# Attention values in 512-column sets, units and gate blocks spread between the projections of an encoder trunk

## The chip, the core and the metric

The kernel runs on one core of one Trainium2 chip. Such a core has TensorE (PE, matrix products into PSUM), VectorE (DVE, elementwise work and reductions), ScalarE (ACT, activations and copies), GpSimd (POOL) and SyncE (SP, which here issues nearly all DMA transfers). SBUF is the working memory with 128 partitions; PSUM holds products in banks of 128 x 512 float32.

The metric is the device time of one execution in microseconds (us); for a kernel it is the median of several runs. A profile is of one execution.

## What is computed

Two layers of an encoder trunk for 512 tokens and a model width of 1024, all in float32. In a layer three mixers run on the same normalized input and are merged by gates, then come a feed-forward part and a gated per-layer input:

```python
h = rmsnorm(x, norm_mix[i])
proj = h @ w_in[i]
qa, ka, va, glu_in, qc, kc, vc, gates = jnp.split(proj, SPLITS, axis=-1)
ya = diff_attention(qa, ka, va, ...)          # 4 heads of two 64-wide halves, values 128 wide
yb = conformer_conv(glu_in, conv_w[i], ...)   # z = a * sigmoid(g), 31 taps, layernorm, silu
yc = neighbourhood_attention(qc, kc, vc, rpb[i])   # 8 heads of 64, on an 8 x 64 grid
ga, gb, gc = jnp.split(jax.nn.sigmoid(gates), 3, axis=-1)
merged = ga * (ya @ w_br_a[i]) + gb * (yb @ w_br_b[i]) + gc * (yc @ w_br_c[i])
x = x + merged @ w_o[i]
h = rmsnorm(x, norm_ffn[i])
x = x + (silu(h @ w_ffn_gate[i]) * (h @ w_ffn_up[i])) @ w_ffn_down[i]
h = rmsnorm(x, norm_ple[i])
x = x + sigmoid(h @ w_ple_gate[i]) * (p[i] @ w_ple_in[i])
```

After the two layers a last `rmsnorm` gives the output. The widths that matter below: `va` and `vc` are 512 columns each, `glu_in` is 2 x 512, `gates` is 3 x 1024.

## The kernel before

**Numbers in two parts.** A float32 operand is kept as a high part (type fp32r, a copy by ScalarE) and a low part (the rest, a subtraction by VectorE); `split` (L162) makes both. A product of two operands is three products on TensorE: high by high, high by low, low by high (`mm3`, L175). `weights` (L166) loads a block of 128 x 1024 weights by SP into a `wr` buffer and splits it into `wh` and `wl`, three buffers of each, with a higher priority than the work around it.

**A projection** is `gemm` (L181): 8 blocks of the contraction, three products each, 24 products of 512 columns (the tokens) into one PSUM bank, which another engine then empties. Activations lie transposed, so a projection gives 128 channels by 512 tokens. `values` (L561) is the exception: it gives tokens by channels, 128 tokens at a time, with the activations as the stationary operand and the weights as the moving one. It makes 256 columns (half of the heads) in a call, 96 products of 256 columns into two banks, and is called four times in a layer: `natten_v(0)`, `natten_v(1)`, `diff_v(0)`, `diff_v(1)`.

**The order of the work.** TensorE's instructions run in the order in which the program issues them (a manual schedule). The order on the other engines is found by a scheduler when the kernel is built, by priority (mostly the order in the program) and by when inputs and buffers come free; within an engine it is then fixed. A buffer has a tag with a number of copies (L293): `v` 4, `y` 5, `z` 5, `x` 4, `t` 7, `rp` 2, `qk` 2, `b` 2, `r` 3, `a` 3, `e` 2; of the eight PSUM banks `mm` has 3, `sc` 2, `tr` 2 and `av` 1.

**Ticks.** Attention is cut into units that are put between the projections. `chunk` (L115) is called after each three products of a projection, and every fourth call is a tick (`tick`, L94): 12 products of 512 columns. At a tick those generators go on whose time has come (`yield 2` is two ticks later), and one more unit is started from the queue. `later(gen, delay, gap)` puts a unit in the queue: it starts at the earliest `delay` ticks later, and the next one at the earliest `gap` ticks after it.

- `natten_in(pr)` projects q and k of two of the 8 neighbourhood heads. SP copies the parts into the stacked buffers `qk` and `x` (12 copies). Four units follow, `natten_unit` (L643): scores on TensorE (`natten_sc`, L762), bias and minimum on VectorE, the exponential on ScalarE; two ticks later transposes (`natten_tr`, L683 to L687), split by ScalarE and VectorE into `natten_pt`; two ticks later the product with the values (`natten_av`, L704 and L705) in the one `av` bank, which ScalarE and VectorE empty into `natten_y`. Two units of a half share the bank. L705 uses edge values, which SP copies to the other partitions after `values`.
- `diff_in(head)` does the same for a head of the differential attention, with the rotary embedding between (VectorE, and four copies by SP for each of q and k). Its units are `diff_unit` (L796): scores (`diff_sc`, L762), and for every second unit three ticks later transposes and two ticks after that `diff_av`, also in the `av` bank, then a norm at the end of a head.

**A layer** (L413): four gated blocks of the convolution's input (`glu`, two projections each), which start before the norm's row factors `rb` are known and are scaled by them on the way out of PSUM. `scaled` (L241) then makes eight normalized operands h[0] to h[7] on VectorE and ScalarE, one a tick; all later projections use these. Then head pair 0 of the neighbourhood attention, `natten_v(0)`, pairs 1 and 2, `natten_v(1)`, pair 3, differential head 0, `diff_v(0)`, head 1, one gate block of the third kind (`gate_c`), head 2, `diff_v(1)`, head 3, the other seven `gate_c`, two `gate_b`, all sigmoids so far, `branch_c` (8 blocks of 12 products), two `gate_b`, `merge_a` (8 x 36 products), and the convolution's norm between four `gate_b`. The first two gated blocks of the first layer are made in `opening`, while the input loads.

**Convolution taps.** The 124 taps of a layer (31 for each of four blocks `z`) are one VectorE instruction each (L160, `conv_z`). They are not placed by the program's order alone: `background(after, n)` (L515) issues the next `n` of them and lets them start no sooner than `after`. `BG` (L51) has the numbers for each kind of work; `conv` issues what is left before it takes the mean.

## Time and profile before

| | |
|---|---|
| median of 3 runs | 1796.83 us (1795.61 to 1800.21) |
| the profiled execution | 1793.92 us |
| its span, first to last instruction | 1792.1 us |
| TensorE busy | 1778.6 us, 10404 products |
| VectorE busy | 1381.7 us |
| ScalarE busy | 895.0 us |
| TensorE's granted clock | 1.000 |
| read from HBM | 216.44 MB, 125 GB/s with what is written |

How it is read: a tile is named by its phase and tag, so `natten_pt` is a buffer of tag `pt` that the phase `natten` made, and an instruction is written out<-in. L12 is line 12 of the kernel; a line can be that of a helper, such as L143 (any activation), L157 (any `tensor_tensor`) or L177 to L179 (the three products of `mm3`). In the timeline a row has the start, the length, the engine and what it does; `x3` are three instructions of one kind merged, and brackets give how long the engine stood idle before it and what ended that. Products are pipelined: the next one starts before the one ahead is drawn to end. In the waits view a row has who waited, for whom, the total in us, how many times, and the longest. In the stages below, layer 0 lies at 28 to 438 us up to the merge, and the same stage of layer 1 some 888 us later.

### The profile page before, as it was taken

Reading aid. Unit: us, or ns where it says so; the run is one execution under the profiler, and the core shown is the slowest. Engines: PE = TensorE matmul, PEld = TensorE weight load, DVE = VectorE, ACT = ScalarE, POOL = GpSimd, SP = SyncE. Lnnn points to the kernel's source line nnn. Section 1 sums busy time; section 2 is a strip of 40 time slices with the busy share of each in tenths; the row PEclk is TensorE's granted clock in tenths of the full one; section 3 lists DMA queues with packets and bytes.
Section 4 is the critical chain, followed back from the end, with each engine's and each line's share of the span. In section 5 each row is a group of like instructions: output and inputs, shape, how many; then the busy total and the mean of one; then the engine's idle time right before and its main releaser. Section 6 shows DMA issues by size and latency. Waiting matters only on the chain. (4 is left out here: it accounts for less than half of the span.)

```text
span 1792.1 us, 27370 instructions
## 1 busy us (share of the span) xinstructions
PE 1778.6 (99%) x10404; PEld 1571.3 (88%) x10404; DVE 1381.7 (77%) x2142; ACT 895.0 (50%) x1499; POOL 63.5 (4%) x102
## 2 busy tenths in 40 slices
PE   9999999999999999999999999999999999999998
PEld 7888888888899899898878888888888998998987
DVE  7888887897877577577787878878878775765776
ACT  5576555325565245255545755553256652542544
POOL 0000000000000000000000000000000100000000
PEclk9999999999999999999999999999999999999999
DMA  6666561325656466253437655523364762763432
GB/s 201 171 191 167 145 159 42 111 90 156 214 142 185 138 155 187 83 140 120 159 117 194 187 152 161 128 63 100 97 192 146 194 180 84 195 169 112 118 111 92
DMA packets 98963, 257.56 MB, mean 144 GB/s; under 512 B 13072, under 2 KB 18576, under 8 KB 98832
## 3 DMA queue, kind: packets, MB, share of 16 engines
q1 hardware_dynamic: 91344, 231.19, 42.4%
q0 software_dynamic: 6336, 23.07, 7.3%
q8 instruction: 82, 1.34, 0.3%
q10 hardware_dynamic: 1152, 1.55, 0.3%
q14 instruction: 49, 0.40, 0.1%
HBM read 216.44 MB, written 7.86 MB: 125 GB/s over the span
## 5 line engine op out<-in xcount | busy, mean ns | idle before, releaser
L143 ACT ACTIVATE ffn_wh<-ffn_wr 128x1024 fp32r<-128x1024 f32 (+1 forms) x114 | 117.3, 1029 | 184.1 <-PE ffn_mm L178 99.5
L160 DVE SCALAR_TENSOR_TENSOR conv_z<-glu_z,pre_par,conv_z 128x512 f32<-128x512 f32 x240 | 179.2, 747 | 2.9
L157 DVE TENSOR_TENSOR ffn_wl<-ffn_wr,ffn_wh 128x1024 fp32r<-128x1024 f32 (+1 forms) x114 | 134.9, 1183 | 49.9 <-ACT ffn_wh L143 49.5
L1049 PE MATMUL ffn_sc<-wo_h,ffn_wh 128*128 128x256 f32 x704 | 130.4, 283 | 0.0
L1049 PEld LDWEIGHTS ffn_sc<-wo_h,ffn_wh 128*128 128x128 f32 x704 | 110.4, 192 | 0.8
L1049 PE MATMUL ffn_sc<-wo_h,ffn_wl 128*128 128x256 f32 x352 | 99.6, 283 | 0.0
L177 PE MATMUL ffn_mm<-ffn_z,ffn_wh 128*128 128x512 f32 x240 | 93.4, 389 | 0.0
L178 PE MATMUL ffn_mm<-ffn_z,ffn_wh 128*128 128x512 f32 x240 | 93.4, 389 | 0.0
L179 PE MATMUL ffn_mm<-ffn_z,ffn_wl 128*128 128x512 f32 x240 | 93.4, 389 | 0.0
L157 DVE TENSOR_TENSOR ffn_t<-ffn_mm,wo_r 128x512 f32<-128x512 f32 x48 | 33.1, 689 | 67.8 <-PE ffn_mm L179 67.8
L157 DVE TENSOR_TENSOR ffn_wl<-ffn_rp,ffn_wh 128x1024 fp32r<-128x1024 f32 x44 | 53.7, 1221 | 30.3 <-ACT ffn_wh L143 30.3
L143 ACT ACTIVATE mergea_wh<-mergea_wr 128x1024 fp32r<-128x1024 f32 (+1 forms) x32 | 27.1, 846 | 96.8 <-PE mergea_mm L178 70.8
L1049 PEld LDWEIGHTS ffn_sc<-wo_h,ffn_wl 128*128 128x128 f32 x352 | 67.5, 192 | 0.0
L1049 PE MATMUL ffn_sc<-wo_qk,ffn_wh 128*128 128x256 f32 x352 | 67.1, 283 | 0.0
L1049 PE MATMUL ffn_sc<-wo_v,ffn_wh 128*128 128x256 f32 x352 | 67.1, 283 | 0.0
L1049 PE MATMUL ffn_av<-wo_h,ffn_wh 128*128 128x256 f32 x352 | 65.3, 283 | 0.0
L143 ACT ACTIVATE ffn_wh<-ffn_rp 128x1024 fp32r<-128x1024 f32 x44 | 46.4, 1055 | 29.6 <-PE ffn_mm L178 17.5
L1049 PEld LDWEIGHTS ffn_sc<-wo_qk,ffn_wh 128*128 128x128 f32 x352 | 54.9, 192 | 0.0
L1049 PEld LDWEIGHTS ffn_av<-wo_h,ffn_wh 128*128 128x128 f32 x352 | 54.9, 192 | 0.0
L1049 PEld LDWEIGHTS ffn_sc<-wo_v,ffn_wh 128*128 128x128 f32 x352 | 54.9, 192 | 0.0
L179 PEld LDWEIGHTS ffn_mm<-ffn_z,ffn_wl 128*128 128x128 f32 x240 | 45.1, 188 | 9.3
L178 PEld LDWEIGHTS ffn_mm<-ffn_z,ffn_wh 128*128 128x128 f32 x240 | 45.1, 188 | 9.2
(688 smaller groups left out, 5785.9 us busy)
## 6 DMA issues: line engine op xcount, KB each, us to landing
ffn_wr<-w_gu SPq DMA_DIRECT2D x66, 512.0 KB, 4.3
ffn_e<-w_gu SPq DMA_DIRECT2D x32, 512.0 KB, 3.6
ffn_e<-w_gu POOLq DMA_DIRECT2D x32, 512.0 KB, 7.5
ffn_wr<-w_fd SPq DMA_DIRECT2D x32, 512.0 KB, 4.4
natten_wr<-w_in SPq DMA_DIRECT2D x16, 512.0 KB, 4.6
natten_b<-bias SPq DMA_DIRECT2D x32, 256.0 KB, 2.9
diff_wr<-w_in SPq DMA_DIRECT2D x16, 512.0 KB, 3.8
gatec_wr<-w_in SPq DMA_DIRECT2D x16, 512.0 KB, 4.2
```

Source lines behind the costliest of these rows:

```text
L143: i = self.nc.scalar.activation(out, in_, func, **kw)
L157: return self.nc.vector.tensor_tensor(out, a, b, op)
L160: return self.nc.vector.scalar_tensor_tensor(out, a, s, b, op0, op1)
L177: mm(out, wh, ah, start=first, stop=False)
L178: mm(out, wh, al, start=False, stop=False)
L179: mm(out, wl, ah, start=False, stop=last)
L1049: mm(bank[:, u], w[:, u, kp], t, start=begin and n == 0, stop=False, skip_group_check=True)
```

## The change

What it does, part by part:

- **Values.** `values` makes all 512 columns in one call, so it is called once for the neighbourhood attention and once for the differential attention. It makes four sets of 128 tokens, in three `mm` banks and the `av` bank, with products of 512 columns. The contraction is walked in three steps (blocks 0 and 1, 2 and 3, 4 to 7), each over all four sets; each set is split as soon as its last product is done. The weights lie in memory in another order; the loads are as many and as large. All four `v` buffers hold one call. The edge values go to four `t` buffers in place of two `x`.
- **Units.** In place of delay 5 and gap 1, a neighbourhood head pair has delays 6, 4, 4, 4 and gaps 2, 2, 2, 1. In place of delay 7 or 6 and gap 2, a differential head has delay 8 (head 0) or 5, and gap 2, for head 3 gap 1.
- **The last gated block** moves from the start of the layer to between head pairs 1 and 2. It uses h, ScalarE copies both projections from PSUM, and `finish` applies the sigmoid and the product after the gate blocks.
- **Gate blocks** are spread: two `gate_c` after pair 2, one after differential head 0, `diff_v` after head 1, `gate_c` and two `gate_b` after head 2, and the rest after head 3. All four `gate_b` that came before `merge_a` now come before `branch_c`, in buffers of tags `b` and `rp`.
- **Taps.** Gated blocks of the first layer and its head pair 0 no longer issue taps, and the second call of a block in `merge_a` issues three in place of two.

```diff
...
 WARM = 10
-BG = dict(glu=2, natten=3, diff=1, gatec=2, branchc=1, gateb=5, mergea=4, mergea2=2)
+BG = dict(glu=2, natten=3, diff=1, gatec=2, branchc=1, gateb=5, mergea=4, mergea2=3)
 FIRST = (["v"] * 4 + ["pt"] * 2 + ["y", "b"], ["y"] * 5 + ["pt"] * 2 + ["b"])
...
         self.todo = self.taps(zs, cs)
-        self.glu(zs)
+        self.glu(zs, range(3))
         if i == 0:
...
         yc, ya, yb = [], [], []
+        acc, gb = [], []
+        self.ms = iter(range(KD)), iter(range(KD))
         sn, sd = {}, {}
...
         self.h = self.hs
-        self.natten_v(0, sn)
+        self.natten_v(sn)
         self.natten_in(1, sn, yc)
+        finish = self.glu_last(zs)
         self.natten_in(2, sn, yc)
-        self.natten_v(1, sn)
+        self.gates(acc, gb, "cc")
         self.natten_in(3, sn, yc)
-        acc, gb = [], []
         self.diff_in(0, sd, ya)
-        self.diff_v(0, sd)
+        self.gates(acc, gb, "c")
         self.diff_in(1, sd, ya)
-        self.gate_c(acc, 0)
+        self.diff_v(sd)
         self.diff_in(2, sd, ya)
-        self.diff_v(1, sd)
+        self.gates(acc, gb, "cbb")
         self.diff_in(3, sd, ya)
-        for m in range(1, KD):
-            self.gate_c(acc, m)
-        for m in range(2):
-            self.gate_b(gb, m, AF.Copy, None)
+        self.gates(acc, gb, "ccbbcc")
         for g in acc + gb:
             self.act(g, g, AF.Sigmoid, table="sigmoid")
+        finish()
         self.branch_c(acc, yc)
-        for m in range(2, 4):
-            self.gate_b(gb, m, AF.Sigmoid, "sigmoid")
         self.merge_a(ya, acc)
...
         return ps
-    def glu(self, zs):
+    def glu(self, zs, js):
         self.phase = "glu"
-        if not self.first:
+        if 0 in js and not self.first:
             self.first = [self.ps("mm") for _ in range(2)]
             self.pair(self.first, [self.a["w_in"][self.i, (OFF_GLU + o) // P] for o in (CB, 0)], self.h)
-        nc = self.nc
-        for j in range(4):
+        for j in js:
             sg, ta = self.sb("t", [P, 512]), self.sb("t", [P, 512])
...
             def value(j=j, pa=pa, sg=sg, ta=ta, z=z):
                 self.tt(ta, pa, self.rb, ALU.mult)
-                mid = z[:, HALO:HALO + GW, :]
-                zc = self.tt(mid.rearrange("p a b -> p (a b)"), ta, sg, ALU.mult)
-                nc.vector.memset(z[:, 0:HALO, 0:1], 0.0)
-                nc.vector.memset(z[:, HALO + GW:, GR - 1:GR], 0.0)
-                nc.vector.tensor_copy(z[:, 0:HALO, 1:GR], z[:, GW:GW + HALO, 0:GR - 1])
-                nc.vector.tensor_copy(z[:, HALO + GW:, 0:GR - 1], z[:, HALO:2 * HALO, 1:GR])
-                if j:
+                zc = self.gated(z, ta, sg)
+                if j and self.i:
                     self.background(zc, self.bg["glu"])
             self.ready(value)
+    def gated(self, z, a, g):
+        nc = self.nc
+        mid = z[:, HALO:HALO + GW, :]
+        zc = self.tt(mid.rearrange("p a b -> p (a b)"), a, g, ALU.mult)
+        nc.vector.memset(z[:, 0:HALO, 0:1], 0.0)
+        nc.vector.memset(z[:, HALO + GW:, GR - 1:GR], 0.0)
+        nc.vector.tensor_copy(z[:, 0:HALO, 1:GR], z[:, GW:GW + HALO, 0:GR - 1])
+        nc.vector.tensor_copy(z[:, HALO + GW:, 0:GR - 1], z[:, HALO:2 * HALO, 1:GR])
+        return zc
+    def glu_last(self, zs):
+        self.phase = "glu"
+        sg = self.sb("r", [P, 512])
+        z = self.sb("z", [P, GW + 2 * HALO, GR])
+        zs.append(z)
+        mid = z[:, HALO:HALO + GW, :].rearrange("p a b -> p (a b)")
+        for out, off in ((sg, CB), (mid, 0)):
+            self.act(out, self.proj(OFF_GLU + off + 3 * P), AF.Copy)
+        def finish():
+            self.act(sg, sg, AF.Sigmoid, table="sigmoid")
+            self.gated(z, mid, sg)
+        return finish
     def taps(self, zs, cs):
...
     def values(self, ap, parts):
         mm = self.nc.tensor.matmul
-        accs = [self.ps("mm", (P, 2, 256)) for _ in range(2)]
-        for o in range(0, KD, 4):
-            wh, wl = self.weights(ap[:, o * 256:(o + 4) * 256], 1024)
-            for k in range(o, o + 4):
-                s = slice((k - o) * 256, (k - o + 1) * 256)
-                for t in range(4):
-                    out = accs[t // 2][:, t % 2, :]
-                    ts = slice(t * P, (t + 1) * P)
-                    mm(out, self.h[k][:, 0, ts], wh[:, s], start=k == 0 and t % 2 == 0,
-                       stop=False, skip_group_check=True)
-                    mm(out, self.h[k][:, 0, ts], wl[:, s], start=False, stop=False,
-                       skip_group_check=True)
-                    mm(out, self.h[k][:, 1, ts], wh[:, s], start=False,
-                       stop=k == KD - 1 and t % 2 == 1, skip_group_check=True)
+        accs = [self.ps("mm") for _ in range(3)] + [self.ps("av")]
+        ws = []
+        def products(t, ks):
+            ts = slice(t * P, (t + 1) * P)
+            for k in ks:
+                wh, wl = ws[k // 2]
+                s = slice(k % 2 * 512, k % 2 * 512 + 512)
+                hi, lo = self.halves(self.h[k])
+                mm(accs[t], hi[:, ts], wh[:, s], start=k == 0, stop=False)
+                mm(accs[t], hi[:, ts], wl[:, s], start=False, stop=False)
+                mm(accs[t], lo[:, ts], wh[:, s], start=False, stop=k == KD - 1)
                 self.chunk()
-                self.chunk()
-        vs = []
-        for acc in accs:
-            v = self.sb("v", [P, 2, 512], F32R)
-            for t in range(2):
-                for hi, lo, a in parts(v[:, t], acc[:, t]):
-                    self.split(hi, lo, a)
-            vs.append(v)
-        return vs
+        for o in range(4):
+            ws.append(self.weights(ap[:, o * 1024:(o + 1) * 1024], 1024))
+        for ks in ((0, 1), (2, 3), (4, 5, 6, 7)):
+            for t in range(4):
+                products(t, ks)
+                if ks[-1] == KD - 1:
+                    v = self.sb("v", [P, 2, 512], F32R)
+                    for hi, lo, a in parts(v, accs[t]):
+                        self.split(hi, lo, a)
+                    accs.append(v)
+        return accs[4:]
     def natten_in(self, pr, st, ys):
...
             self.background(self.stt(low, ps, f, nat.bitcast(F32), ALU.mult, ALU.subtract),
-                            self.bg["natten"])
+                            self.bg["natten"] if pr or self.i else 0)
             self.stack(nat, low, st4[:, 2 * s:2 * s + 2], k2 if s else None)
...
         for n in range(4):
-            self.later(self.natten_unit(pr, n // 2, n % 2, st4, k2, st, box, ys[pr]), 5, 1)
+            self.later(self.natten_unit(pr, n // 2, n % 2, st4, k2, st, box, ys[pr]),
+                       (6, 4, 4, 4)[pr], (2, 2, 2, 1)[pr])
     def stack(self, nat, low, one, two):
...
                                                part[64 * u:64 * u + 64].bitcast(F32))
-    def natten_v(self, g, st):
+    def natten_v(self, st):
         self.phase = "natten"
         def parts(v, a):
-            v = v.rearrange("p (u a b c) -> p u a b c", u=2, b=2, c=64)
-            a = a.rearrange("p (u a c) -> p u a c", u=2, c=64)
-            return [(v[:, u, :, u], v[:, u, :, 1 - u], a[:, u]) for u in range(2)]
-        vs = self.values(self.a["w_vc"][self.i, g], parts)
-        vd = self.sb("x", [P, 2, 512], F32R)
-        for n, edge in enumerate((vs[1][0:64, 0], vs[0][64:P, 1])):
-            for o in range(0, P, 64):
-                self.nc.sync.dma_start(vd[o:o + 64, n].bitcast(F32), edge.bitcast(F32))
-        st["v", g] = vs, vd
+            v = v.rearrange("p g (u a b c) -> p u g a b c", u=2, b=2, c=64)
+            a = a.rearrange("p (g u a c) -> p u g a c", g=2, u=2, c=64)
+            return [(v[:, u, :, :, u], v[:, u, :, :, 1 - u], a[:, u]) for u in range(2)]
+        vs = self.values(self.a["w_vc"][self.i], parts)
+        vds = []
+        for g in range(2):
+            vds.append([self.sb("t", [P, 512], F32R) for _ in range(2)])
+            for vd, edge in zip(vds[g], (vs[2][0:64, g], vs[1][64:P, g])):
+                for o in range(0, P, 64):
+                    self.nc.sync.dma_start(vd[o:o + 64].bitcast(F32), edge.bitcast(F32))
+        st["v"] = vs, vds
     def natten_unit(self, pr, half, u, st4, k2, st, box, y):
...
         yield 2
-        vs, vd = st["v", pr // 2]
+        vs, vds = st["v"]
+        g = pr // 2
         if u == 0:
...
             for k in range(2):
-                mm(av, vs[half][:, n, cols], pp[:, k, n], start=n == k == 0, stop=False)
-        mm(av[:, ws], vd[:, half, cols], p2, start=False, stop=True)
+                mm(av, vs[2 * half + n][:, g, cols], pp[:, k, n], start=n == k == 0, stop=False)
+        mm(av[:, ws], vds[g][half][:, cols], p2, start=False, stop=True)
         qs = slice(half * 256, half * 256 + 256)
...
         self.tt(y[rs, 1, qs], y[rs, 1, qs].bitcast(F32), av[ro], ALU.add)
+    def gates(self, acc, gb, names):
+        for n in names:
+            if n == "c":
+                self.gate_c(acc, next(self.ms[0]))
+            else:
+                self.gate_b(gb, next(self.ms[1]), AF.Copy, None)
     def gate_c(self, acc, m):
...
         if m % 2 == 0:
-            gs += self.parts_of("v", [512], 2)
+            if m == 0:
+                gs += [self.sb("b", [P, 512]) for _ in range(2)]
+            else:
+                gs += self.parts_of("rp" if m == 2 else "v", [512], 2)
         self.background(self.act(gs[m], ps, func, table=table), self.bg["gateb"])
     def merge_b(self, ys, acc, gs):
...
         for qt in range(4):
-            self.later(self.diff_unit(head, qt, st4, k2, st, box, ys), 6 if head else 7, 2)
-    def diff_v(self, g, st):
+            self.later(self.diff_unit(head, qt, st4, k2, st, box, ys), 8 if head == 0 else 5,
+                       1 if head == 3 else 2)
+    def diff_v(self, st):
         self.phase = "diff"
-        st["v", g] = self.values(self.a["w_va"][self.i, g], lambda v, a: ((v[:, 0:256], v[:, 256:512], a),))
+        def parts(v, a):
+            return [(v[:, :, 0:256], v[:, :, 256:], a.rearrange("p (g c) -> p g c", g=2))]
+        st["v"] = self.values(self.a["w_va"][self.i], parts)
     def diff_unit(self, head, qt, st4, k2, st, box, ys):
...
             for u in range(2):
-                v = st["v", head // 2][kp][:, u].rearrange("p (a b) -> p a b", a=2)
+                v = st["v"][2 * kp + u][:, head // 2].rearrange("p (a b) -> p a b", a=2)
                 self.mm3(av[:, half * 256:half * 256 + 256], v[:, 0, cs], v[:, 1, cs],
...
 def _vblocks(w):
-    w = w.reshape(L, KD, P, 2, 256).transpose(0, 3, 2, 1, 4)
-    return np.ascontiguousarray(w).reshape(L, 2, P, KD * 256)
+    w = w.reshape(L, KD, P, 512).transpose(0, 2, 1, 3)
+    return np.ascontiguousarray(w).reshape(L, P, KD * 512)
 def _heads(w):
```

## Prediction

> **What bounds the kernel now.** First the head of the page, then the windows view over stretches of one kind of work, then the list of waits on TensorE.

> ```profile
> span 1792.1 us, 27370 instructions
> PE 1778.6 (99%) x10404; PEld 1571.3 (88%) x10404; DVE 1381.7 (77%) x2142; ACT 895.0 (50%) x1499; POOL 63.5 (4%) x102
> ```

> TensorE is busy for 99% of the span, so only two things shorten the kernel: fewer or cheaper products, or fewer waits between them. The windows view gives the price of a product (a stretch, its length, TensorE's busy time and products, the granted clock, the share and rate of DMA):

> ```profile
> 61.84:73.34 11.50, 11.50 (x97) 1.00 0.73 209
> 340.82:406.10 65.28, 65.28 (x290) 1.00 0.30 91
> 61.84:137.59 75.75, 73.52 (x476) 1.00 0.71 195
> ...
> 950.00:1023.55 73.55, 73.10 (x475) 1.00 0.72 200
> ```

> The first row is the first call of `values`: 96 products of 256 columns begin in it (the 97th is a neighbour that reaches in), one every 11.50/96 = 119.8 ns. The second is merge A: 8 x 36 = 288 products of 512 columns, one every 65.28/288 = 226.7 ns. So two products of 256 columns take 239.6 ns and one of 512 takes 226.7, at a granted clock of 1.00 in both.

> The last two rows are the same stretch of both layers (from the neighbourhood values to the first projection of the differential attention): the first layer takes 2.2 us longer for the same products, so part of this stage is waiting. The list of waits has these in it:

> ```profile
> PE natten_tr L683 <- DVE natten_pt L157: 1.3, 2, 0.7
> ...
> PE natten_av L704 <- DVE natten_y L157: 1.0, 3, 0.4
> ...
> PE natten_sc L762 <- DMA natten_x<-natten_t: 0.8, 1, 0.8
> PE natten_sc L762 <- DMA natten_qk<-natten_t: 0.6, 1, 0.6
> ```

> This view counts a wait only from the drawn end of the product before. A 512-column product is drawn 0.39 us long and the next one may start after 0.227, so 0.16 us of each such wait is hidden. Start against start in the timeline shows the whole of it:

> ```profile
> 75.86 0.39 PE L179 MATMUL natten_mm<-glu_h,natten_wl 128*128 128x512 f32 x1
> 76.88 0.38 PE L762 MATMUL natten_sc<-natten_qk 128*128 128x256 f32 x1 [0.62 <-DMA natten_qk<-natten_t]
> 78.08 0.39 PE L762 MATMUL natten_sc<-natten_x,natten_qk 128*128 128x256 f32 x1 [0.82 <-DMA natten_x<-natten_t]
> ```

> ```profile
> 99.88 0.39 PE L179 MATMUL natten_mm<-glu_h,natten_wl 128*128 128x512 f32 x1
> 100.64 0.71 PE L704 MATMUL natten_av<-natten_pt,natten_v 128*128 128x256 f32 x4 [0.36 <-DVE natten_y L157]
> ```

> ```profile
> 144.92 0.22 PE L705 MATMUL natten_av<-natten_a,natten_x 128*128 128x128 f32 x1
> 145.79 0.30 PE L683 MATMUL natten_tr<-pre_ident,natten_e 128*128 128x128 f32 x1 [0.66 <-DVE natten_pt L157]
> ```

> ```profile
> 130.89 0.39 PE L179 MATMUL natten_mm<-glu_h,natten_wl 128*128 128x512 f32 x1
> 131.27 0.35 PE L704 MATMUL natten_av<-natten_pt,natten_v 128*128 128x256 f32 x1
> ```

> The first scores lose 1.02 - 0.23 = 0.79 and 1.20 - 0.12 = 1.08 us to the DMAs that stack q and k, once, in the first layer. `natten_av` loses 0.76 - 0.23 = 0.53 us to a PSUM bank that VectorE has not emptied (three such, 1.0 + 3 x 0.16 = 1.5). The transposes lose 0.87 - 0.06 = 0.81 us (two such, 1.6). The last pair of rows is a wait of 0.38 - 0.23 = 0.15 us which shows no idle time at all. With 0.4 in the scores of `diff_sc` (rows in point 7) the visible waits come to 1.9 + 1.5 + 1.6 + 0.4 = 5.4 us. For hidden ones like the last I take ten, 1.5 us, as an estimate (bounds 0 and 3). Together about 7.0 us.

> **The change, part by part.** The sum is made against the profiled execution, 1793.92 us, of which 1792.1 are its span. It lies 2.9 us under the median of the runs, 1796.83, so the difference is taken from the median.

> *Products.* `values` runs four times in a layer with 96 products of 256 columns, and afterwards twice with 96 of 512: 768 x 119.8 ns = 92.0 us become 384 x 226.7 = 87.0. That is 5.0 us less, on the engine that sets the end. Projections, units, weight loads (8 of 512 KB a layer before and after) and the edge copies (8 a layer) stay equal in number; evictions become fewer and wider. The fourth gated block moves two evictions from VectorE to ScalarE (50% busy), which I cost at nothing.

> [...]

> *Waits removed.* Units of head pairs 0 to 2 start every second tick (a tick is 12 products of 512 columns, 2.7 us) and not every one. The transposes and `natten_av` that waited then have a full 24 products, 5.4 us, between a unit and the next, while the whole wait was under 1 us. I count all of the 7.0 us as removed, and what may come back as new waits.

> *New waits.* I count the order of products from the code.

> 1. The `av` bank. `diff_v` takes three `mm` banks and the single `av` bank for its fourth set, whose first product stands 6 products (1.4 us) behind the last product of the last neighbourhood unit. All queued after it on TensorE wait with it. That unit's bank is free when VectorE has added into `natten_y`:

> ```profile
> 183.92 0.22 PE L705 MATMUL natten_av<-natten_a,natten_x 128*128 128x128 f32 x1
> ```

> ```profile
> 189.33 0.42 DVE L157 TENSOR_TENSOR natten_y<-natten_y,natten_av 64x256 fp32r<-64x256 f32 x1
> ```

> ```profile
> 149.75 0.22 PE L705 MATMUL natten_av<-natten_a,natten_x 128*128 128x128 f32 x1
> ```

> ```profile
> 150.87 0.42 DVE L157 TENSOR_TENSOR natten_y<-natten_y,natten_av 64x256 fp32r<-64x256 f32 x1
> ```

> From 1.5 us after it (150.87 + 0.42 - 149.75) to 5.8 us (this very unit, behind the rotary work of a head). Less 1.4 that is 0.1 to 4.4 us a layer. In the new order rotary work ended a tick earlier and no scores compete, so I take 1.0 a layer: 2.0.

> 2. The first `diff_av` wants the same bank 16 products (3.6 us) after `diff_v` ends. Splits of a whole call were ready 3.7 to 7.1 us after it (rows of point 3); here one set is left: 0 to 3.5 a layer, 0.2 taken: 0.4.

> 3. The edge copies. The first neighbourhood unit's last product needs set 2 of the values split, copied by SP and landed, 9.6 us after that set's products end. Before, the copies were issued 3.7 to 7.7 us after the first call ended at 73.34:

> ```profile
> 77.00 1.10 SPq L640 DMA_DIRECT2D natten_x<-natten_v  x2
> 80.09 0.33 SPq L650 DMA_DIRECT2D natten_b<-bias  x1
> 80.47 1.10 SPq L640 DMA_DIRECT2D natten_x<-natten_v  x2
> ```

> With some 3 us to land (the last stacking copy, the row of 74.08 below, freed the product at 78.08) that is 7 to 12 us: 0 to 2.2 a layer, 0.5 taken: 1.0.

> 4. The values start 10.9 us sooner, since two projections of the gated block left. Their third set needs the bank of k0's projection 2.7 us after it ends, and the operands h[4] to h[7] about 11 us after the start:

> ```profile
> 61.32 1.41 DVE L160 SCALAR_TENSOR_TENSOR natten_t<-natten_mm,glu_r 128x512 f32<-128x512 f32 x2
> ```

> ```profile
> 64.09 0.74 DVE L160 SCALAR_TENSOR_TENSOR glu_h<-pre_x,pre_par,glu_h 128x512 fp32r<-128x512 f32 x1
> ```

> The first row evicts q0's and k0's banks, at 61.32 and 62.0. k0 ended at 61.84, q0 24 products (5.4 us) before it, so the waits were 0.9 and 4.9 us: 0 to 2.2, 0.4 taken. h[7], the second row, was ready at 64.83. It is wanted 57 products (12.9 us) after the start, at about 63.9, and five taps and the gated block's evictions (some 7 us of VectorE) no longer stand ahead of it: 0.

> 5. The first scores: 72 products (16.3 us) behind k0, where before the second copy let them go at 78.08 - 61.84 = 16.2. 0 to 2, 0.5 taken.

> 6. Convolution taps. In the first layer 54 and not 42 are left for merge A:

> ```profile
> 340.82:406.10 65.28, 33.69 (x45) 1.00 0.30 91
> ```

> ```profile
> 340.82:406.10 65.28, 65.28 (x290) 54.05 (x289) 57.69 (x78) 17.73 (x26) 0.00 (x0) 1.00 0.30 91
> ```

> The first row is L160 on VectorE alone, 33.69/45 = 0.75 us a tap. VectorE's 57.7 us (the third busy figure of the second row) become 57.7 + 9 = 66.7 of 65.3; two ticks (5.4 us) of other products follow before the mean of the convolution is wanted. 0 to 2, 0.5 taken.

> 7. Head 3 of the differential attention starts a unit each tick. Its scores want banks that ScalarE must have read, as here:

> ```profile
> 1079.35 0.39 PE L762 MATMUL diff_sc<-diff_x,diff_qk 128*128 128x512 f32 x1
> 1080.01 0.50 PE L762 MATMUL diff_sc<-diff_qk 128*128 128x512 f32 x1 [0.28 <-ACT diff_e L143]
> ```

> 0.66 - 0.23 = 0.43 us for each of three, so 0 to 1.3 a layer, 0.2 taken: 0.4.

> 8. Reordering of ScalarE and VectorE that I can't follow: 0 to 2, 1.0 taken.

> New waits: 2.0 + 0.4 + 1.0 + 0.4 + 0.5 + 0.5 + 0.4 + 1.0 = 6.2 us. **Sum**: -5.0 - 7.0 + 6.2 = -5.8 us, 1788.1 for the profiled execution's like and 1791.0 for the median.

> **The rivals.**

> *The waits go and nothing comes for them.* All chains fit their ticks: -12, 1785. For it: each chain that waited did so by less than 1 us. Against: one `av` bank now serves three users.

> *The bank hand-over gives the gain back.* Waits 1 and 3 at their upper ends: 2 x (4.4 + 2.2) = 13.2 in place of 3.0, so -5.8 + 10.2 = +4.4 at the worst; at half of that, 1796. For it the 5.8 us of the very unit that stands ahead of the bank.

> *Slower: SP behind a weight load.* The four weight blocks of `values` share three buffers, and the last two are held to its end. The raw load of a later block stands in SP's queue until a buffer is free, and the stacking copies of head pairs 0 and 1 behind it:

> ```profile
> SPq L171 <- DVE natten_wl L157: 21.6, 5, 5.2
> ```

> ```profile
> 70.18 0.33 SPq L171 DMA_DIRECT2D natten_wr<-w_vc  x1
> ...
> 74.08 1.24 SPq L621 DMA_DIRECT2D natten_x<-natten_t  x2
> ```

> One such wait is up to 5.2 us, and the first scores have no slack (point 5). One for each of two head pairs in two layers is 4 x 5.2 = 20.8 less 6 us for the slack of the second pair: -5.8 + 14.8 = +9, 1806. It decides once copies are held for more than 3 us a pair. Against it: h and the order of loads stay the same, and the units have one tick more.

> [...]

> **How the numbers follow.** Forecast 0.46, nothing comes 0.15, bank hand-over 0.22, SP 0.14, no fixed cost 0.03. The predicted time is 1791. The range reaches to the second case's 1785 less 2 for the spread of single runs, and over the hand-over's 1796 up to 1800, short of the SP case: 1783 to 1800. A measurement tells a change from none at about 0.3%, 5.4 us, so faster is below 1791.4: three quarters of the forecast (0.35) and all of the second case, 0.50; slower, above 1802.2, is the SP case, 0.14; between, 0.36.

> **What would show it.** The 384 products of `values` in 87.0 us; no `natten_av` or `natten_tr` among the waits for head pairs 0 to 2; a wait of about 1 us on `natten_y` at the first product of `diff_v`'s fourth set; SP's copies of head pair 0 landed before the first scores. The prediction is wrong if waits on TensorE in the two attention stages exceed 7 us, or if merge A or the convolution's mean waits for taps by more than 2 us.

## The result and the profile after

The changed kernel takes 1808.2 us (median of 4 runs, 1807.98 to 1811.4) where the kernel before takes 1797.3 beside it: a ratio of 1.0074, 95% interval 1.0059 to 1.0089. It is slower by about 0.7%; 1791 was forecast, in a range up to 1800. The profiled executions, from which all that follows is read, have 1807.98 us here and 1793.92 before; their spans lie 14.1 us apart, the medians 10.9.

The head of the page after:

```profile
span 1806.2 us, 26575 instructions
PE 1779.0 (98%) x10020; PEld 1555.2 (86%) x10020; DVE 1371.2 (76%) x2114; ACT 897.3 (50%) x1483; POOL 63.6 (4%) x102
```

384 products are gone (10404 less 10020), as the change says, and yet TensorE is busy no less and the span is 14.1 us longer. All of that lies ahead of merge A: its first product begins at 348.9 us against 340.8 before, from there to the one of layer 1 it is 892.8 us against 886.5, and what follows is as long as before (564.5 against 564.8). The price of a product of `values` is as forecast. The windows view over 24 of them in `diff_v` (length, busy time of TensorE, weight loads, VectorE, ScalarE and GpSimd, the granted clock, share and rate of DMA):

```profile
204.11:209.55 5.44, 5.44 (x25) 4.50 (x24) 4.11 (x8) 2.40 (x6) 0.00 (x0) 1.00 0.85 214
```

5.44/24 = 226.7 ns (the 25th is a neighbour reaching in). So the loss lies between the products. The list of waits on TensorE after (total, how many, the longest):

```profile
PE natten_sc L794 <- DVE natten_s L680: 5.7, 2, 2.8
PE diff_sc L794 <- DMA diff_x<-diff_rp: 3.8, 2, 2.2
PE natten_av L726 <- DVE natten_y L157: 3.7, 4, 1.6
PE natten_mm L592 <- DVE natten_t L160: 1.6, 1, 1.6
...
PE diff_av L177 <- DVE diff_v L157: 0.9, 2, 0.4
PE diff_sc L794 <- ACT diff_pt L143: 0.9, 1, 0.9
```

No `natten_tr` is among them, and the four `natten_av` all belong to head pair 3: the old waits of pairs 0 to 2 are gone. In their place stand four new places, called A to D from here on. Their lengths are counted from start to start: the time from the start of the product ahead to the start of the one that waited, less the pitch, which is what this step takes without a wait (0.227 us behind 512 columns).

**A**, the scores of the second unit of pair 3, 3.00 us beyond the pitch in each layer (behind the products at 161.72 and 1055.73). The timeline of TensorE and VectorE there:

```profile
159.06 1.23 DVE L157 TENSOR_TENSOR diff_wl<-diff_wr,diff_wh 128x1024 fp32r<-128x1024 f32 x1 [1.93 <-ACT diff_wh L143]
...
161.57 0.68 DVE L157 TENSOR_TENSOR diff_rp<-diff_rp,diff_r 128x512 f32<-128x512 f32 x1
161.72 0.39 PE L179 MATMUL gatec_mm<-glu_h,gatec_wl 128*128 128x512 f32 x1
162.18 0.74 DVE L160 SCALAR_TENSOR_TENSOR conv_z<-glu_z,pre_par,conv_z 128x512 f32<-128x512 f32 x1
162.84 0.68 DVE L157 TENSOR_TENSOR diff_rp<-diff_rp,diff_r 128x512 f32<-128x512 f32 x1
...
163.86 0.69 DVE L157 TENSOR_TENSOR diff_rp<-diff_rp 128x512 f32<-128x512 f32 x1
164.47 0.42 DVE L680 CUSTOM_DVE_ANT_0 natten_b<-natten_sc,natten_b 128x256 f32<-128x256 f32 x1
...
164.95 0.58 PE L794 MATMUL natten_sc<-natten_qk 128*128 128x256 f32 x1 [2.84 <-DVE natten_s L680]
```

The scores need a bank that the minimum (L680) of the unit before must have read. In VectorE's fixed order it stands behind a weight split for which VectorE waited 1.93 us, and behind head 0's rotary work (`diff_rp`) and a tap.

**B**, `natten_av` of pair 3 (0.49 and 1.71 in layer 0, 0.47 and 1.71 in layer 1), held by the `av` bank that VectorE empties late. The rows of the longer one:

```profile
189.12 1.23 DVE L157 TENSOR_TENSOR diff_wl<-diff_wr,diff_wh 128x1024 fp32r<-128x1024 f32 x1 [0.97 <-ACT diff_wh L143]
...
190.92 0.69 DVE L157 TENSOR_TENSOR diff_rp<-diff_rp,diff_r 128x512 f32<-128x512 f32 x1
191.52 0.41 DVE L157 TENSOR_TENSOR natten_y<-natten_av,natten_y 64x256 fp32r<-64x256 f32 x1
191.86 0.67 DVE L157 TENSOR_TENSOR diff_rp<-diff_rp 128x512 f32<-128x512 f32 x1
192.56 0.42 DVE L157 TENSOR_TENSOR natten_y<-natten_y,natten_av 64x256 fp32r<-64x256 f32 x1
193.13 0.71 PE L726 MATMUL natten_av<-natten_pt,natten_v 128*128 128x256 f32 x4 [1.55 <-DVE natten_y L157]
```

The emptying stands behind a weight split for which VectorE waited 0.97 us, a tap and head 1's rotary work. Ahead of the shorter wait (0.49, ended by the row at 183.64) stands such a split too, at 181.26 behind 0.99 us of idle time, but no rotary work.

**C**, the first scores of head 3 (2.45 + 0.36 + 0.17 and 1.05 + 1.87), held in the main by its key copies. SP's and TensorE's rows:

```profile
291.25 1.24 SPq L640 DMA_DIRECT2D diff_x<-diff_rp  x2
...
294.57 0.79 PE L794 MATMUL diff_sc<-diff_x,diff_qk 128*128 128x512 f32 x1 [2.20 <-DMA diff_x<-diff_rp]
```

The copies were issued 0.65 us ahead of the first scores (291.90). **D**, k0's bank at the third set of the neighbourhood values, 1.81 once (`natten_mm` in the list of waits).

The second loss is in the granted clock, which before was 1.00 as long as products ran. Windows of 3.41 us from 160.90 on:

```profile
160.90:164.31 3.41, 1.21 (x6) 0.67 (x4) 3.33 (x7) 0.00 (x0) 0.00 (x0) 1.00 0.70 210
164.31:167.72 3.41, 2.77 (x9) 2.38 (x10) 3.40 (x13) 2.88 (x9) 0.00 (x0) 0.50 0.45 105
167.72:171.14 3.42, 3.42 (x10) 2.65 (x9) 1.60 (x4) 0.87 (x4) 0.00 (x0) 0.50 0.81 226
171.14:174.55 3.41, 3.41 (x24) 3.08 (x23) 2.46 (x4) 3.34 (x7) 0.15 (x1) 1.00 0.15 34
```

In the third row TensorE never waits, and yet eight products begin in it, most of them 0.427 us apart, where the 3.41 us would hold 15 (3.41/0.227). (The view counts ten, since two reach in from the row above.) Behind wait A in layer 0 the clock is halved for 6.83 us, and behind C, A and C again for 3.41 us each: 17.1 us in all while products run (behind the last one the end of the span is at 0.50 too, 3.5 us here and 1.6 before). Less the 1.55 us of waiting in them, 0.47 of the rest is lost (1 - 0.227/0.427): 7.3 us.

The account: A 6.0, B 4.4, C 5.9, D 1.8, smaller ones 2.1 (0.61 twice at the first `diff_av`, 0.44, 0.47), half clock 7.3: 27.5 us of new loss. Less 4.8 for the products that leaves 22.7, and measured are 14.1. The difference, 8.6 us, is what must have gone with the old waits. A count of every step against the median pitch of its kind, in the stages ahead of merge A, agrees within a microsecond: 15.8 us in the trace of before and 35.7 after, 19.9 more, so that 27.5 - 19.9 = 7.6 us have gone.

### The profile page after: what moved, and what is told of

It reads as the page before. It is cut to its first block, busy times and chain, and to the rows that moved or that the text cites. A ratio compares the mean times of both kernels' runs of the same rounds, so it can differ in the third digit from the quotient of the medians.

```text
span 1806.2 us, 26575 instructions
## 1 busy us (share of the span) xinstructions
PE 1779.0 (98%) x10020; PEld 1555.2 (86%) x10020; DVE 1371.2 (76%) x2114; ACT 897.3 (50%) x1483; POOL 63.6 (4%) x102
## 3 DMA queue, kind: packets, MB, share of 16 engines
q10 hardware_dynamic: 1152, 1.55, 0.3%
## 5 line engine op out<-in xcount | busy, mean ns | idle before, releaser
L143 ACT ACTIVATE ffn_wh<-ffn_wr 128x1024 fp32r<-128x1024 f32 (+1 forms) x114 | 117.2, 1028 | 183.2 <-PE ffn_mm L178 103.7
L160 DVE SCALAR_TENSOR_TENSOR conv_z<-glu_z,pre_par,conv_z 128x512 f32<-128x512 f32 x240 | 179.3, 747 | 2.7
L157 DVE TENSOR_TENSOR ffn_wl<-ffn_wr,ffn_wh 128x1024 fp32r<-128x1024 f32 (+1 forms) x114 | 134.9, 1183 | 45.3 <-ACT ffn_wh L143 44.8
L179 PE MATMUL ffn_mm<-ffn_z,ffn_wl 128*128 128x512 f32 x240 | 93.4, 389 | 0.0
L157 DVE TENSOR_TENSOR ffn_t<-ffn_mm,wo_r 128x512 f32<-128x512 f32 x48 | 33.0, 689 | 72.9 <-PE ffn_mm L179 72.8
L157 DVE TENSOR_TENSOR ffn_wl<-ffn_rp,ffn_wh 128x1024 fp32r<-128x1024 f32 x44 | 53.7, 1221 | 30.1 <-ACT ffn_wh L143 30.1
L143 ACT ACTIVATE mergea_wh<-mergea_wr 128x1024 fp32r<-128x1024 f32 (+1 forms) x32 | 27.1, 847 | 87.9 <-PE mergea_mm L178 80.4
L1086 PE MATMUL ffn_av<-wo_h,ffn_wh 128*128 128x256 f32 x352 | 65.3, 283 | 0.0
L143 ACT ACTIVATE ffn_wh<-ffn_rp 128x1024 fp32r<-128x1024 f32 x44 | 46.4, 1056 | 29.4 <-PE ffn_mm L178 17.5
L891 DVE TENSOR_REDUCE diff_s<-diff_sc 128x1 f32<-128x512 f32 x64 | 43.0, 684 | 22.4 <-PE diff_sc L794 22.2
L143 ACT ACTIVATE natten_e<-natten_b,natten_s 128x256 f32<-128x256 f32 x64 | 32.1, 502 | 44.3 <-issue 38.8
```

What stands on the lines that cost most here:

```text
L143: i = self.nc.scalar.activation(out, in_, func, **kw)
L157: return self.nc.vector.tensor_tensor(out, a, b, op)
L160: return self.nc.vector.scalar_tensor_tensor(out, a, s, b, op0, op1)
L179: mm(out, wl, ah, start=False, stop=last)
L891: nc.vector.tensor_reduce(out=m[:, u:u + 1], in_=sc, op=ALU.max, axis=AX.X, negate=True)
L1086: mm(bank[:, u], w[:, u, kp], t, start=begin and n == 0, stop=False, skip_group_check=True)
```

## The experiments

Kernels are named by a number; a diff is against the changed kernel if nothing else is said, and "before" is timed beside each group (medians 1795.0 to 1797.3).

**e1: head 3's units two ticks later** (wait C).

```diff
-8 if head == 0 else 5, 1 if head == 3 else 2
+(8, 5, 5, 7)[head], 1 if head == 3 else 2
```

> The changed kernel with delay 7 in place of 5 for head 3 of the differential attention. Theory (three chains given too few ticks, and the granted clock at 0.5 for a while after each wait of 2 to 3 us): the first scores of head 3 no longer wait for the stacked copies of k (2.8 us in each layer before), and the two stretches at 0.5 behind them (3.4 us each, half lost) go: about 5.6 + 3.4 = 9 us less than the changed kernel, so 1799. Rival (the wait only moves to the next step, the sigmoids or branch c): less than 3 us gained, above 1805.

1801.2 us (ratio 1.0034, 1.0021 to 1.0047), 7.0 us less. C is gone and so are both half-clock stretches behind it; in exchange head 3 now waits 0.57 and 0.72 us at `diff_av` in each layer. Not all of the 7.0 us are C's: A has its 3.0 us in both layers here, but half clock follows it for 3.41 us in layer 0, where it was 6.83, and not at all in layer 1, where it was 3.41. The delay of head 3 was not meant to do that. The windows around both, the first row of layer 0 with half clock, the others of layer 1:

```profile
166.33:169.75 3.42, 3.42 (x10) 2.64 (x9) 3.38 (x10) 2.15 (x8) 0.00 (x0) 0.50 0.70 165
```

```profile
1050.39:1053.80 3.41, 2.18 (x10) 1.48 (x8) 3.40 (x7) 0.49 (x2) 0.00 (x0) 1.00 0.52 130
1053.80:1057.21 3.41, 1.80 (x9) 1.58 (x10) 3.34 (x14) 1.91 (x6) 0.00 (x0) 1.00 0.43 138
1057.21:1060.63 3.42, 3.42 (x23) 3.08 (x22) 3.28 (x6) 3.40 (x9) 0.15 (x1) 1.00 0.88 222
```

In the trace of the changed kernel the half-clock stretches begin at 164.31, 294.02, 1058.60 and 1188.31, the last three 38, 262 and 300 times 3.413 us behind the first, and each lasts one or two times that: they lie on one grid. In e1 the windows above lie on the grid of its own stretch (1050.39 is 259 times 3.413 us behind 166.33), and in layer 1 a boundary of it cuts the wait in two: TensorE is busy 2.18 and 1.80 of the 3.41 us. That led to e8.

**e2: the units' minimum, exponential and scale ranked ahead** of other work on VectorE and ScalarE (wait A).

```diff
+with self.soon():      # priority offset 200
     nc.vector.tensor_tensor_reduce(out=b[:, t], in0=sc, ...)
```

> The changed kernel with the minimum, the exponential and the scaling of a neighbourhood unit given a higher priority, so that VectorE and ScalarE have them ahead of the rotary work of head 0. Theory: the second scores of head pair 3 lose their wait of 3.0 us in each layer, and the stretches at clock 0.5 behind it (6.8 and 3.4 us, half lost) go: 6.0 + 5.1 = 11 us less, 1797. Rival (the scores wait for the bias that SP loads, or for a bank, not for the order on VectorE): the waits stay at 3.0 us and the time within 2 us of 1808.

1808.6 (1.0077, 1.0062 to 1.0092): no gain. The wait at the scores is gone and stands one step on, at the transposes of the same unit:

```profile
170.40 0.39 PE L179 MATMUL diff_mm<-glu_h,diff_wl 128*128 128x512 f32 x1
174.50 0.45 PE L712 MATMUL natten_tr<-pre_ident,natten_e 128*128 128x128 f32 x1 [3.71 <-DVE natten_pt L157]
```

The minimum came early and the emptying of the transposes late. Rank of one step of the unit is not the cure.

**e3: each product of `values` as two of 256 columns; e4: waits put into merge A of the kernel before** (a chain of VectorE products ahead of a transpose).

> The changed kernel with each product of values as two products of 256 columns. By the pitches of the profile before (119.8 and 226.7 ns) the products of values take 5.0 us longer, and if no wait changes the kernel is at 1813. [...] More time for the chains could hide some of the waits in diff_v, up to 2 us.

> The kernel before with a chain of VectorE products behind each block of merge A, of 1 to 6 links, and a transpose on TensorE that waits for it: eight waits of about 1 to 4 us in each layer, each followed by 36 products. Theory (a single wait of 2.5 to 3 us lowers the granted clock for 3.4 us or more): the clock stays at 1.0 behind the waits under 2 us and shows stretches of 3.4 us at 0.5 behind those over 2.5 us. Rival (the clock fell for the sum of many waits in a stage, not for one): stretches at 0.5 also behind short ones, or none at all.

e3: 1812.0 (1.0097, 1.0079 to 1.0114), 3.8 more than the changed kernel, where the rows' 5.0 were expected; its half-clock stretches differ (10.2 us of them, not 17.1; the mean granted clock is 0.996, not 0.994), so e20 repeats it in a kernel that has none (e19, mean clock 0.999). e4, a single run: 1923.3. The waits came out longer than meant, 3.0 to 8.0 us, and half clock came with them: the mean granted clock is 0.975 of a span of 1921.6 us, which is some 96 us at 0.50. So it says nothing of waits under 2 us.

**e8: shorter waits in merge A of the kernel before**, to see what halves the clock.

```diff
+for n in ((128,), (256,), (384,), (512,), (512, 128), (512, 256), (512, 384), (512, 512))[m]:
+    self.nc.vector.tensor_copy(q[:, 0:n], pb[:, 0:n])
+self.nc.tensor.transpose(self.ps("tr", (P, P)), q[:, 0:P], self.ident)
 self.tt(g, g, pb, ALU.mult)
```

> The kernel before, with a transpose behind each of the eight merge A blocks of a layer that waits for one or two VectorE copies of 128 to 1024 columns: sixteen waits between about 1.5 and 2.9 us, at whatever point of the grid of 3.413 us they fall. Theory: the granted clock is 0.5 in the stretch of 3.413 us that follows one in which TensorE stood idle for more than about 1.87 us, and in no other, so a wait of 2.5 us that a boundary cuts in two halves does nothing. Rival: the length alone decides, every wait above some 2.4 us is followed by 0.5 and none below. Time: 16 waits of some 2.2 us and some half-clock stretches of 1.7 us each: 1830 to 1850.

1827.8, a single run, just under the 1830 to 1850 expected. A wait of 2.63 us at 385.33 fell across a boundary, one of 2.77 at 396.31 inside a window:

```profile
382.86:386.27 3.41, 2.86 (x13) 2.04 (x11) 2.62 (x4) 1.81 (x3) 0.00 (x0) 1.00 0.28 53
386.27:389.69 3.42, 1.50 (x7) 1.30 (x8) 3.21 (x6) 0.31 (x1) 0.00 (x0) 1.00 0.45 166
389.69:393.10 3.41, 3.41 (x16) 2.81 (x15) 2.50 (x4) 0.00 (x0) 0.00 (x0) 1.00 0.03 11
...
396.52:399.93 3.41, 0.80 (x5) 0.56 (x5) 3.10 (x6) 1.05 (x1) 0.00 (x0) 1.00 0.40 144
399.93:403.34 3.41, 3.41 (x10) 2.64 (x9) 3.31 (x5) 0.00 (x0) 0.00 (x0) 0.50 0.14 38
```

The wait of 2.77 is followed by half clock; that of 2.63 is not, nor is e1's of 3.00 in layer 1, which is longer than both. So the rival, that the length alone decides, is out; what a window of the grid held went with the clock here. The expectation's 1.87 us of idle time were an estimate, and no sharp edge: the window from 386.27 on has 1.91 (3.41 - 1.50) with full clock behind it, and one of the changed kernel, from 290.60 on, has 1.83 (3.41 - 1.58) with half clock behind it.

**e5: units of all pairs a tick apart** (the spacing undone); **e6: gate blocks behind pair 3's projection; e7: e6 with e1 and another order of banks** (D).

```diff
 # e5
-(2, 2, 2, 1)[pr]
+1
 # e6 and e7
-self.gates(acc, gb, "cc"); self.natten_in(3, sn, yc); self.diff_in(0, sd, ya); self.gates(acc, gb, "c"); self.diff_in(1, sd, ya)
+self.natten_in(3, sn, yc); self.gates(acc, gb, "ccc"); self.diff_in(0, sd, ya); self.diff_in(1, sd, ya)     # and gaps (2, 2, 1, 1)
 # e7: banks of natten_v
-mm, mm, mm, av
+mm, mm, av, mm
```

> The changed kernel with neighbourhood units a tick apart for all head pairs, as before, in place of two ticks for pairs 0 to 2. Theory: the spacing is what removed the old waits, so natten_tr and natten_av of pairs 0 to 2 wait again in some six places of 0.5 to 0.8 us, 3 to 5 us together, while the waits of pair 3 stay: 1811 to 1813 us. Rival: they went because the values are one call, whose products stand between the units: no new wait, 1808.

> The changed kernel with the three gate blocks that stand around head pair 3's projection and head 0's put together behind pair 3's projection, and pair 2's units a tick apart, so that pair 3's units run beside gate blocks and head 0 and are through before the rotary work of head 1. Theory: the waits of pair 3 (3.00 and 2.99 at its second unit's scores; 0.49 + 1.71 and 0.47 + 1.71 at natten_av) come from rotary work on VectorE at the same time; they go, and with them 10.2 us at half clock behind them: 1808.2 - 6.0 - 4.4 - 5.1 = 1792.7, up to 2 us more for pair 2: 1793 to 1795. Rival: units one tick apart are too much for VectorE by themselves, the waits move to pairs 2 and 3 at their new place: 1806 to 1810.

> The kernel e6, and with it head 3's units two ticks later as in e1, and the av bank for the third set of the neighbourhood values in place of the fourth, so that the bank of k0's projection is wanted 6 products later. Theory: the three causes add up: e6's 1793 to 1795, less 7.0 (e1: 1801.2 against 1808.2), less 1.4 of the 1.81 at the bank of k0: 1785 to 1787, with no stretch at half clock. Rival: e1 and e6 shift the same VectorE work, the waits come back elsewhere and the sum is not reached: 1792 to 1796.

e5: 1813.2 (1.0097, 1.0080 to 1.0114), 5.0 more: waits of 0.45 to 0.55 at `natten_av` of pairs 0 to 2 come back, and one of 1.70 for an edge copy. The spacing is what keeps these away. The old waits at `natten_tr` of pairs 0 to 2 do not come back with it, so what removed them is not shown. The 5.0 us are a net figure: in place of A transposes wait 2.77 and 2.87, `diff_v`'s fourth set waits 0.84 in each layer, and the half clock is down from 17.1 to 10.2 us (mean granted clock 0.996, not 0.994).

e6: 1821.1 (1.0139, 1.0122 to 1.0157), which neither side expected. `natten_av` of pair 3 still waits (1.12 and 1.72, then 1.68 and 2.32), and heads 0 and 1 now follow each other:

```profile
189.99 0.39 PE L593 MATMUL diff_mm<-diff_wh,glu_h 128*128 128x512 f32 x1
198.62 0.79 PE L591 MATMUL diff_mm<-diff_wh,glu_h 128*128 128x512 f32 x1 [8.25 <-ACT diff_rp L143]
```

Each projection of a head is evicted into `rp`, of which there are two. Four in a row outrun the rotary work, and `diff_v` wants the bank of the one that can't be evicted. In the changed kernel the block between the two heads gives the rotary work that time. e7: 1814.4 (1.0103, 1.0088 to 1.0118), 6.8 less than e6, where the two parts should have brought 8.4; 0.45 is left of D's 1.81, and e6's waits are all there (8.17 and 8.12 at `diff_v`).

**e12, e13, e14: three ways at A and B**, all with e1 and e7's banks. e12 puts `diff_v` between heads 0 and 1 and moves gate blocks; e13 ranks whole units of pairs 2 and 3 first (offset 450); e14 ranks weight loads and splits 60 instructions ahead, not 400.

> e1, with the av bank for the third set of the neighbourhood values as in e7, and the differential values back between heads 0 and 1 (where the kernel before had a half of them); pair 3's projection and three gate blocks stand ahead of head 0, gate blocks 'cb' behind heads 1 and 2. Base: e1 1801.2 less 1.4 for k0's bank = 1799.8. Theory: rotary work of one head, not of two, meets pair 3's units, and rotary buffers have the values' time to come free, so e6's wait of 8.4 us at diff_v goes, and of the waits at pair 3 (6.0 and 4.4, with 1.7 of half clock) at most a third stays: 1790 to 1793. Rival: the rotary work of head 0 alone is enough for natten_av waits of 3 us a layer as in e6: 1797 to 1801.

> Base as in e12 (1799.8), the order of the changed kernel, and every VectorE and ScalarE instruction of the units of pairs 2 and 3 ranked ahead of weight splits and rotary work, not only the scores as in e2. Theory: waits A (3.00 and 2.99, with 1.7 of half clock) and B (2.2 a layer) are a matter of what stands ahead in VectorE's order, so they go, and the rotary work, with over 10 us of slack, takes them: 1788 to 1791. Rival: VectorE and ScalarE have too much there, and the wait moves on once more, to a weight split or a rotary copy: 1798 to 1803.

> Base as in e12 (1799.8), the order of the changed kernel; weight loads and splits from the neighbourhood values to the last gate block are ranked 60 instructions ahead of their place in place of 400. Theory: VectorE stands idle 1.93 us ahead of wait A for a weight split whose buffer is not free; ranked later it doesn't stand in front of the units, so A loses about 1.9 us in each layer and with it the half clock: 1794. Rival: the order of the splits is set by when their buffers come free and hardly changes, or the splits come too late for TensorE (waits on wl or wh): 1799 to 1806.

All three miss their times. e12: 1827.9 (1.0178, 1.0161 to 1.0195). The waits for the minimum fall to 0.6 and 0.8, but `natten_av` of pair 3 still loses 2.8 and 4.0 us a layer, as its rival had it; `diff_av` waits 4.46 and 4.43 for head 3, and a later head's scores 3.8 and 4.3 for copies. e14: 1807.7 (1.0067, 1.0052 to 1.0082). The rank did not move the split it was aimed at:

```profile
158.78 1.23 DVE L157 TENSOR_TENSOR diff_wl<-diff_wr,diff_wh 128x1024 fp32r<-128x1024 f32 x1 [1.93 <-ACT diff_wh L143]
```

VectorE stands idle for the same 1.93 us, and A grows to 3.75, so how much of A is the split's stays open. e13: 1810.4 (1.0080, 1.0065 to 1.0095); A and most of B are gone and the wait has moved on to the eviction of head 1's keys, 4.7 and 4.8 us:

```profile
194.43 0.80 PE L592 MATMUL diff_mm<-diff_wh,glu_h 128*128 128x512 f32 x1 [4.55 <-ACT diff_rp L143]
```

Also pairs 0 and 1, which were not ranked up, wait 0.6 to 1.4 at their transposes.

**e15, e16, e17: head 0 sooner**, on the same base as e12 to e14. One gate block goes from ahead of pair 3's projection to behind head 0's; units of pair 3 keep their ticks. e16 keeps pair 2 at two ticks; e17 adds the rank for pair 3's units alone.

```diff
-self.gates(acc, gb, "cc"); self.natten_in(3, sn, yc); self.diff_in(0, sd, ya); self.gates(acc, gb, "c")
+self.gates(acc, gb, "c"); self.natten_in(3, sn, yc); self.diff_in(0, sd, ya); self.gates(acc, gb, "cc")
-delays (6, 4, 4, 4), gaps (2, 2, 2, 1); head delays (8, 5, 5, 7)
+delays (6, 4, 4, 6), gaps (2, 2, 1, 1); head delays (10, 5, 5, 7)      # e16: (6, 4, 4, 4), (2, 2, 2, 1)
```

> Base as in e12 (1799.8). One gate block moves from ahead of pair 3's projection to behind head 0's, so that head 0's rotary work is over two ticks (5.4 us) sooner against pair 3's units, which keep their ticks, and heads 0 and 1 stay apart by two blocks; pair 2's units a tick apart. Theory: wait A (3.00 and 2.99 us and 1.7 of half clock) is head 0's rotary work standing ahead of pair 3's second unit: it goes, 7.7 us; B (2.2 a layer, head 1's rotary work) stays: 1792. Rival: what stands ahead is not head 0's rotary work but the general load, and a wait of the same size shows at pair 2 or 3: 1798 to 1802.

> As e15 with pair 2's units two ticks apart as in the changed kernel. Theory: the queries of pair 2 are held two to three ticks longer, so head 0's stacking copies wait for that buffer in SP's queue (up to 5 us) and later loads with them: 1792 to 1797, not faster than e15. Rival: pair 2's spacing is what keeps its units from waiting, and this is the faster of the two: 1790.

> As e15, with the VectorE and ScalarE instructions of pair 3's units alone ranked ahead of splits and rotary work. Theory: with head 0's rotary work out of the way there is room, so B goes as well (4.4 us) and nothing comes for it: 1788. Rival: the wait moves to the eviction of head 1's key projection, 4.7 us in each layer as in e13: 1797 to 1801.

e15: 1801.2 (1.0037, 1.0023 to 1.0050). A is down to 0.6 in both layers and there is no half clock left while products run (mean granted clock 0.999), but pair 2, a tick apart beside head 0, now waits 0.47 and 2.31 at `natten_av` and 0.54 at scores in each layer. That is the time and the place of the rival, a wait of the same size at pair 2. Its reason, the general load, is not what VectorE's rows show there:

```profile
154.15 1.23 DVE L157 TENSOR_TENSOR diff_wl<-diff_wr,diff_wh 128x1024 fp32r<-128x1024 f32 x1 [1.87 <-ACT diff_wh L143]
155.29 0.69 DVE L157 TENSOR_TENSOR diff_rp<-diff_rp,diff_r 128x512 f32<-128x512 f32 x1
...
158.20 0.42 DVE L157 TENSOR_TENSOR natten_y<-natten_y,natten_av 64x256 fp32r<-64x256 f32 x1
```

A split with idle time ahead of it and the rotary work of head 0, as they stood ahead of pair 3's minimum in A, now stand ahead of pair 2's emptying of the `av` bank. The collision went along with head 0, as the theory has it; it did not go away. e16: 1801.0 (1.0032, 1.0020 to 1.0043), the time of neither side; a wait of 3.4 at the transposes of pair 3 in each layer, one with half clock (mean granted clock 0.997). e17: 1798.7 (1.0021, 1.0011 to 1.0032); pair 2's waits are as in e15, and what pair 3 gains goes in part to the bank at `diff_v`'s fourth set (0.93 in each layer). Its time is in the rival's range by luck: the rival's wait, at head 1's keys, is not there.

**e18, e19: rank for pair 2 too; head 3 spaced.**

```diff
 # e18 against e17
-with self.soon(450 if pr > 2 else 0):
+with self.soon(450 if pr > 1 else 0):
+plan.insert(4, plan.pop(3))       # diff_v: the fourth set begins 6 products later
 # e19 against e18
-(10, 5, 5, 7)[head], 1 if head == 3 else 2
+(10, 5, 5, 6)[head], 2
```

> e17 with the units of pair 2 ranked first as well as those of pair 3, and the first products of diff_v's fourth set 6 products later, behind the second group of its first set. Theory: e17's waits of pair 2 at natten_av (0.46 + 2.32 and 0.54 at scores, in each layer) are the same matter of rank, 5.6 us together with the scores' 1.1 over both layers, and the bank's 0.93 in each layer is gone with 1.4 us more: 1798.7 - 6.6 - 1.8 = 1790.3, faster than before. Rival: ranking pair 2 first too pushes head 0's rotary work behind its slack, and the eviction of a diff projection waits as in e13: 1797 to 1803.

> e18 with head 3's units two ticks apart and a tick sooner (delay 6, gap 2). Theory: the waits of head 3 (diff_av 0.57 + 0.72 and diff_sc 0.62 or 0.48 in each layer) come from its spacing of one tick: 3.6 us less than e18: 1786.7. Rival: the last unit ends only at the first product of merge A that reads it and waits there, or the first scores meet the copies again: not faster than e18.

Both come out as the theory has it: e18 1790.65 (0.9963, 0.9951 to 0.9975), e19 1787.1 (0.9946, 0.9934 to 0.9958), 0.5% faster than the kernel before. e18 makes two edits at once, and what each is worth was not separated. The waits of e19, cut to those in the attention stages:

```profile
PE natten_av L737 <- DVE natten_y L158: 3.7, 6, 1.0
...
PE diff_av L178 <- DVE diff_v L158: 0.9, 2, 0.5
PE diff_sc L805 <- DMA diff_x<-diff_rp: 0.8, 2, 0.5
...
PE natten_mm L593 <- DVE natten_t L161: 0.3, 1, 0.3
```

**e20: e19 with products of 256 columns; e21: the kernel before with e18's rank.**

> e19 with each product of values as two of 256 columns in the same places, where no half-clock stretch and few waits blur it as in e3. Theory: 384 pairs at 239.6 ns in place of one at 226.7, 5.0 us more than e19's 1787.1: 1792. [...]

> The kernel before with the rank that e18 gives to the units of pairs 2 and 3 and nothing else: how much of e19's gain the order alone would have given to the kernel before. Theory: the kernel before has only some 2 us of such waits in pairs 2 and 3 (natten_tr 0.81 at 145.79 and parts of natten_av 1.5), so at most 2 us: 1795 to 1797. Rival: the rank pushes its rotary work behind its slack as in e13, and it is slower: 1800 to 1806.

e20: 1792.9 (0.9988, 0.9979 to 0.9997), its span 5.1 us longer than e19's. The same 24 products of `diff_v` in e19, and as 48 in e20:

```profile
197.30:202.74 5.44, 5.44 (x26) 4.50 (x24) 4.08 (x8) 2.45 (x6) 0.00 (x0) 1.00 0.93 263
```

```profile
198.40:204.14 5.74, 5.74 (x49) 5.74 (x48) 3.98 (x7) 2.49 (x6) 0.00 (x0) 1.00 0.82 226
```

0.30 us in 24, times 16, is 4.8 us; the median is 5.8 us over e19's, and a wait for copies at head 3's scores, 0.42 us in e19 and 1.52 here, has about the rest. e21: 1810.4 (1.0079, 1.0067 to 1.0092): the rank by itself makes the kernel before slower, with waits of 2.9 at `natten_tr` and 2.1 at `natten_av` in each layer and half clock behind the first (0.50 from 1023.52 to 1026.93 in layer 1, 0.997 on the mean of the run). So the rank is not by itself what makes e18 and e19 faster; it helped where head 0 had been moved (e17, e18) and not where it had not (e13, e21).

## Why the forecast was wrong

**Products, -5.0: right.** 24 products take 5.44 us, and e20 puts the gain at 4.8. The case that the chances call "no fixed cost" is shown by no run: two products of 256 columns take 12.9 ns more than one of 512 by the rows of before (239.6 and 226.7), and 12.5 more by e20's (0.30 us in 24).

**Waits removed, -7.0: right.** They are gone, and the account leaves 7.6 to 8.6 us for them. That the spacing removed them is shown for `natten_av` alone, by e5.

**New waits, 6.2: the step that failed.** They are 20.2 us, and 7.3 of half clock come behind them. That is also the forecast's own sign of being wrong, more than 7 us of waits in the attention stages.

- Point 8, "reordering of ScalarE and VectorE that I can't follow: 0 to 2", taken as 1.0, held the main term: A and B, 10.4 us. There units of pair 3 stand in VectorE's fixed order behind rotary work of heads 0 and 1, taps, and weight splits for which VectorE itself waits. I had counted the order of products and not the order of VectorE's work, although the forecast knew of this very collision: the row at 189.33 shows pair 3's last unit 5.8 us late behind the rotary work of a head. When e15 moves head 0, all but 0.6 of A goes and the same rows hold up pair 2; e2 shows that the rank of one step is not the cure. Two things stay open: what share the splits have (e14 did not move them), and which part of the re-ordering brought pair 3's units and this work together. That `diff_v` no longer stands between heads 0 and 1 is not shown to be it: e12 puts it back there, and `natten_av` of pair 3 loses more.
- Point 1, the bank at `diff_v`, 1.0 a layer: the hand-over is there, but one step sooner, at pair 3's own `natten_av` (2.2 a layer). The fourth set itself waits only once the units are through sooner (0.93 in e17).
- Point 7 looked at the banks of head 3's scores (0.4, and 0.47 came). It left out that the units start 5 ticks after their projection and not 6 as before, and that the copies need that time: C, 5.9 us, and two of the four half-clock stretches. With 7 ticks C is gone (e1, 7.0 us less, some of it A's half clock); e19, with 6 and two ticks between the units, still waits 0.4 and 0.7 there.
- Point 4, k0's bank, 0.4 of 0 to 2.2: mis-sized: 1.8, inside its bounds; e7's bank order leaves 0.45.
- Points 2, 3, 5 and 6: the first `diff_av` 1.2 where 0.4 was taken; no wait for edge copies or for the first scores, none for taps in merge A.
- The clock was taken as 1.00 for good, as every row of before had it: 7.3 us at a term put at nothing. No wait in the list of before is longer than 1.1 us, and the windows ahead of half clock in the changed kernel have 1.83 us of idle time or more (the least from 290.60 on, 3.41 - 1.58).

**The slower rival** named 1806 and the wrong mechanism: SP's copies of pairs 0 and 1 were in time, and the copies that came late are head 3's. Its time, 2 us off the measured one, is luck. The bank hand-over's 1796 had the right place for B, which is 4.4 of the 27.5 us.

The forecast's idea that the merge pays is right once the rest is put right: with blocks between the heads, the rank of two pairs and head 3's spacing, e19 is at 1787.1, 4 us under the forecast. Of the 10 us that it gains, 4.8 are the products' (e20).
